# Gate and up products of a feed-forward block as one 2x2 block product: seven block products for eight in two of four k groups, weight sums on VectorE, one PSUM pool

## The chip, the cores and the metric

One core of one Trainium2 chip runs the whole kernel as one program. The metric is the device time of one execution in microseconds; before the change its median is 2232.03 us.

## The reference, cut to what matters

Two transformer-like blocks work on 256 tokens of width 2048, in float32. The first is an attention block with three branches (in the reference `first_block`), the second a recurrent block with a retention branch, and it ends in a feed-forward part. Only that feed-forward part matters here. With `u` the normed activations (256 x 2048, gain `ln2` on each feature) it computes

```python
h = silu(u @ w_gate) * (u @ w_up)      # both weights 2048 x 5632
x = x + h @ w_down                     # 5632 x 2048, then a last norm
```

The factor 1/rms of a token is applied after the products (`hr3`, `hr33`), so that the products themselves take `x * ln2`.

## The kernel before, in words

All large products go through one helper, `gemm` (from L133): the output is token-major, two PSUM tiles of 128 tokens x 512 columns (`ps[0]`, `ps[1]`), and the weights stream past in chunks of 512 columns. For each group of four k tiles of 128 rows one DMA on the SP queue brings `raw` (128 x 4 x 512, 1 MB, three buffers). Each float32 operand is split in two float32r parts: for two k tiles at a time ScalarE (ACT) copies `raw` to `hi` (L162, 128 x 1024), VectorE (DVE) computes `lo = raw - hi` (L163, 128 x 1024). Below, such a pair of tiles is called a part; `hi` and `lo` have four buffers each. The left side is split in the same way into tiles with h and l at the end of their names (class `Lhs`, for this stage `lu2`, tiles u20h, u20l to u23h, u23l). A block product (128 tokens x 128 k x 512 columns) is three matmuls: L141 with hi and high, L142 with lo and high, L143 with hi and low. A part therefore feeds 2 k tiles x 2 token halves x 3 = 12 matmuls, a chunk of 512 columns with 16 k tiles 96.

Between the steps of a product, `issue` takes one piece of side work from a queue (transposes, norms, attention pieces). The frame then schedules all instructions by its own priorities and cost model, so that the order on an engine is not the order of the code: DMA issues run ahead, and an engine goes through its list strictly in order.

The feed-forward part (from L881) runs in three parts of 4, 4 and 3 chunks f of 512 columns. Before the change, for each f: `pg = gemm("fg", w_gate, ...)`; ACT forms tanh (L904, `th`), DVE forms `sg = (th + 1) * pg` (L905); then `pu = gemm("fu", w_up, ...)` and DVE multiplies (L908); `next_lhs` transposes `sg` on TensorE (PE; L216, tiles `trm`, eight transposes a chunk) and splits it to ff0h, ff0l and so on (L203, L204). After each part of chunks four products `fd` with `w_down` follow, and DVE adds them to the residual (L918). What is called a chunk below is one f, gate and up together: 192 matmuls and eight transposes.

PSUM has eight banks: four in the pool `mmp` for `gemm`, two in `trp` for transposes, two in `scp` for attention scores. SBUF slots of 4 KB per partition (`slot`, 28 of them) hold the long-lived tiles.

Of the kernel before, what the change touches and what calls it, by code (L numbers as in the profile page):

```python
# [34 lines left out]
# columns of the shape constants  # L35
# [9 lines left out]
def two_blocks(ctx: ExitStack, tc: tile.TileContext, x, xT, mem, memT, w_in, w_mem_kv, w_proj_a,  # L45
# [69 lines left out]
    class Lhs:  # L115
        """Split transposed activations: chunks of four k-tiles, [P, 4, S] high and low parts."""
# [16 lines left out]
    def gemm(name, w, r0, nk, col0, lhs, fine=False, tail=False, rate=1):  # L133
        ps = [mmp.tile([P, 512], F32, tag="mm", name=name) for _ in range(NT)]
# [49 lines left out]
    def rstd_from(ss, name, r=None):  # L184
        # ss [P, n, NCH] -> (mean + eps) ** -0.5, [P, n]
# [91 lines left out]
    def evac_T(ps, r, dst):  # L277
        # token-major chunk scaled by r, transposed: [P feature, 4, S]
# [16 lines left out]
    def evac_silu(ps, hr, name):  # L295
        # silu(r z) without the factor r / 2
# [37 lines left out]
    def prob_tile(name):  # L334
        return tp.tile([P, 768], F32, tag="prob", name=name)
# [4 lines left out]
    def inverse(l, hr, shape, name):  # L340
        # hr / l, for l [P, 2, NT] or [P, NT]
# [8 lines left out]
    # ================= block 1 =================  # L350
# [6 lines left out]
    # memory attention  # L357
# [21 lines left out]
    def mem_attention(lhs, c):  # L379
# [58 lines left out]
    # causal attention, four heads a group  # L438
# [8 lines left out]
    def causal_attention(hi, lo, c, hp, key):  # L447
# [3 lines left out]
        def scores():  # L451
            sc = scp.tile([P, 2, 512], F32, tag="sc", name="sca")
            for i in range(2):
                h = 2 * hp + i
                nc.tensor.matmul(sc[:, i, 0:P], qa[c][:, h, 0:P], ka[c][:, h, 0:P], start=True, stop=True)
                nc.tensor.matmul(sc[:, i, P:3 * P], qa[c][:, h, P:S], ka[c][:, h, :], start=True, stop=True)
            for i in range(2):
                for b in (0, 2):
# [533 lines left out]
```

## Time and profile before

| what | value |
|---|---|
| median of 2 runs | 2232.03 us (2231.84 to 2232.22) |
| span of the profiled execution, first to last instruction | 2229.9 us |
| what lies around the span, median less span | 2.1 us |
| PE busy in the span | 2212.3 us |
| DVE busy | 1262.8 us |
| ACT busy | 1025.0 us |
| HBM read | 418.00 MB |

The span is that of one profiled execution, and every duration below comes from it. A matmul's recorded duration overlaps with the next one's, so the rate of PE is read from the starts of its rows, not from the mean duration. The same holds, to a smaller degree, for DVE and ACT.

### The profile page before, as it was taken

What the parts mean: (1) busy time and instruction counts of PE and PEld (TensorE: products, weight loads), DVE (VectorE), ACT (ScalarE), POOL (GpSimd) and SP (SyncE); (2) the same over time, 40 slices, a digit from 0 to 9 for tenths busy, and PEclk for the clock granted to TensorE, in tenths of its full rate; (3) what the DMA queues carried; (4) which work ended last, traced back from release to release, by engine and by line L of the source; (5) the groups of instructions that cost most, each with busy time, mean ns of one, the idle gap of its engine ahead of it and who ended that gap; (6) DMA issues with size and microseconds to landing.
All of it is one profiled execution on the core that took longest, in us unless ns stands there. A gap on an engine that the chain in (4) does not pass through costs nothing.

```text
span 2229.9 us, 25130 instructions
## 1 busy us (share of the span) xinstructions
PE 2212.3 (99%) x10108; PEld 1833.4 (82%) x10108; DVE 1262.8 (57%) x1531; ACT 1025.0 (46%) x1253; POOL 9.2 (0%) x15
## 2 busy tenths in 40 slices
PE   8999999999999999999999999999999999999998
PEld 6888888888888888888888888888888888888886
DVE  5545555655555455555677777555555555555555
ACT  6644444444444444444554554544444444434443
POOL 0000000000000000000000000000000000000000
PEclk9999999999999999999999999999999999999999
DMA  8755455455555545556665545555555565565554
GB/s 308 261 185 164 152 189 190 158 181 189 189 189 189 180 143 176 195 191 207 212 226 172 186 152 172 188 188 189 189 189 189 191 194 192 185 198 191 189 198 142
DMA packets 215380, 421.72 MB, mean 189 GB/s; under 512 B 6880, under 2 KB 13152, under 8 KB 215264
## 3 DMA queue, kind: packets, MB, share of 16 engines
q1 hardware_dynamic: 214688, 419.08, 57.2%
q8 instruction: 79, 1.29, 0.2%
q10 hardware_dynamic: 576, 1.05, 0.1%
q14 instruction: 37, 0.30, 0.0%
HBM read 418.00 MB, written 2.10 MB: 188 GB/s over the span
## 4 chain that ended last, share of the span: by engine, by line
PE 98%; DMA 0%; ACT 0%; issue 0%; DVE 0%; SPq 0%; POOLq 0%; POOL 0%; ACTq 0%
PE gate L143 4%; PE gate L142 4%; PE gate L141 4%; PE fg L143 4%; PE fg L141 4%; PE fg L142 4%; PE fu L143 4%; PE fu L141 4%; PE fu L142 4%; PE fd L143 4%; PE fd L141 3%; PE fd L142 3%; PE wo L143 3%; PE wo L141 3%; PE wo L142 3%; PE proj L141 2%
## 5 line engine op out<-in xcount | busy, mean ns | idle before, releaser
L163 DVE TENSOR_TENSOR lo<-raw,hi 128x1024 fp32r<-128x1024 f32 (+1 forms) x769 | 939.5, 1224 | 902.0 <-ACT hi L162 901.0
L162 ACT ACTIVATE hi<-raw 128x1024 fp32r<-128x1024 f32 (+1 forms) x769 | 813.7, 1059 | 1096.9 <-PE fu L143 139.6
L141 PE MATMUL gate<-hi,hn1h 128*128 128x512 f32 x96 | 38.5, 401 | 0.0
L141 PE MATMUL gate<-hi,hn0h 128*128 128x512 f32 x96 | 38.5, 401 | 0.0
L141 PE MATMUL gate<-hi,hn2h 128*128 128x512 f32 x96 | 38.4, 400 | 0.0
L141 PE MATMUL gate<-hi,hn3h 128*128 128x512 f32 x96 | 38.3, 399 | 0.0
L142 PE MATMUL gate<-lo,hn1h 128*128 128x512 f32 x96 | 37.6, 392 | 0.0
L143 PE MATMUL gate<-hi,hn0l 128*128 128x512 f32 x96 | 37.6, 392 | 0.0
L143 PE MATMUL gate<-hi,hn1l 128*128 128x512 f32 x96 | 37.5, 391 | 0.0
L142 PE MATMUL gate<-lo,hn2h 128*128 128x512 f32 x96 | 37.5, 391 | 0.0
L143 PE MATMUL gate<-hi,hn2l 128*128 128x512 f32 x96 | 37.5, 391 | 0.0
L143 PE MATMUL gate<-hi,hn3l 128*128 128x512 f32 x96 | 37.5, 391 | 0.0
L142 PE MATMUL gate<-lo,hn0h 128*128 128x512 f32 x96 | 37.5, 391 | 0.0
L142 PE MATMUL gate<-lo,hn3h 128*128 128x512 f32 x96 | 37.5, 391 | 0.0
L141 PE MATMUL fg<-hi,u20h 128*128 128x512 f32 x88 | 35.2, 400 | 0.0
L141 PE MATMUL fg<-hi,u21h 128*128 128x512 f32 x88 | 35.2, 400 | 0.0
L143 PE MATMUL fg<-hi,u20l 128*128 128x512 f32 x88 | 34.5, 392 | 0.0
L143 PE MATMUL fg<-hi,u21l 128*128 128x512 f32 x88 | 34.4, 391 | 0.0
L142 PE MATMUL fg<-lo,u21h 128*128 128x512 f32 x88 | 34.3, 390 | 0.0
L142 PE MATMUL fg<-lo,u20h 128*128 128x512 f32 x88 | 34.3, 390 | 0.0
L143 PE MATMUL fu<-hi,u20l 128*128 128x512 f32 x88 | 34.3, 390 | 0.0
L143 PE MATMUL fg<-hi,u23l 128*128 128x512 f32 x88 | 34.3, 390 | 0.0
(943 smaller groups left out, 5516.0 us busy)
## 6 DMA issues: line engine op xcount, KB each, us to landing
raw<-in_w_in_dram SPq DMA_DIRECT2D x184, 1024.0 KB, 5.2
raw<-in_w_gate_dram SPq DMA_DIRECT2D x44, 1024.0 KB, 5.2
raw<-in_w_up_dram SPq DMA_DIRECT2D x44, 1024.0 KB, 5.2
raw<-in_w_down_dram SPq DMA_DIRECT2D x44, 1024.0 KB, 5.1
raw<-in_w_out_dram SPq DMA_DIRECT2D x32, 1024.0 KB, 5.1
raw<-in_w_mem_kv_dram SPq DMA_DIRECT2D x15, 1024.0 KB, 7.6
raw<-in_w_proj_m_dram SPq DMA_DIRECT2D x8, 1024.0 KB, 5.1
raw<-in_w_proj_a_dram SPq DMA_DIRECT2D x8, 1024.0 KB, 5.1
```

Source lines behind the costliest of these rows:

```text
L141: nc.tensor.matmul(ps[t], xh[:, c], hi, start=(kt == 0), stop=False)
L142: nc.tensor.matmul(ps[t], xh[:, c], lo, start=False, stop=False)
L143: nc.tensor.matmul(ps[t], xl[:, c], hi, start=False, stop=(kt == nk - 1))
L162: A.activation(hi[:, a:b], raw[:, h + a:h + b], AF.Copy)
L163: V.tensor_tensor(out=lo[:, a:b], in0=raw[:, h + a:h + b], in1=f32(hi[:, a:b]), op=ALU.subtract)
```

## The change

The outputs of a chunk f are seen as a 2 x 2 matrix of blocks: token half 0 or 1 by gate or up. In a k group of kind S two k tiles at a time form a 2 x 2 x 2 block product, and this is computed with seven block products instead of eight (the scheme of Strassen and Winograd), with sums and differences on both sides. On the activation side these are formed once, before the feed-forward part (`next_forms`: seven blocks of 128 x 128 per pair of k tiles). On the weight side they are formed for each chunk on DVE: `t1`, `t2`, `t3`, `t4`, each 128 x 1024. All seven weight forms are split into hi and lo. In a k group of kind D there are eight block products as before, but accumulated so that they fit the same banks: bank 3 takes `x0 - x1` (tile `u21d`, `u23d`) times up. The kinds of the four groups are S, D, S, D (`PATTERN`). The seven products have a PSUM bank each; DVE combines them at the end of a chunk with seven operations of 128 x 512 (L322 to L328), and ACT copies one bank (`p1`, L321). All PSUM tiles come from one pool of eight banks; `raw` has four buffers instead of three, there are 26 slots instead of 28, and score tiles are two single banks, so that some reductions and exponentials of the attention stages are two instructions instead of one.

The core of the diff (comments that it removes, and hunks that only rename a PSUM tile, are left out):

```diff
-NSLOT = 28
+NSLOT = 26
+RBUFS = 4
+TBUFS = 2
+PATTERN = "SDSD"
...
-    mmp = ctx.enter_context(tc.tile_pool(name="mmp", bufs=4, space=bass.MemoryType.PSUM))
-    scp = ctx.enter_context(tc.tile_pool(name="scp", bufs=1, space=bass.MemoryType.PSUM))
-    trp = ctx.enter_context(tc.tile_pool(name="trp", bufs=2, space=bass.MemoryType.PSUM))
+    pp = ctx.enter_context(tc.tile_pool(name="pp", bufs=8, space=bass.MemoryType.PSUM))
...
-            raw = wp.tile([P, 4, 512], F32, tag="raw", name="raw", bufs=3)
+            raw = wp.tile([P, 4, 512], F32, tag="raw", name="raw", bufs=RBUFS)
...
+        def piece(h):
+            k1, k2 = 2 * h, 2 * h + 1
+            a = a_tile("fa", 8)
+            order = (((1, k1), (0, k1), (0, k2), (1, k2)) if kind == "S" else
+                     ((0, k1), (1, k1), (0, k2), (1, k2)))
+            ty = transposed("trm", [block(t, k) for t, k in order])
+            for i, k in ((0, k1), (1, k2)):
+                A.activation(flat(a[:, 2 * i:2 * i + 2]), ty[:, i * S:(i + 1) * S], AF.Copy, scale=gains[:, k:k + 1])
+            if kind == "S":
+                for o, i0, i1 in ((4, 0, 3), (5, 1, 4), (6, 2, 5), (7, 0, 1)):
+                    V.tensor_tensor(out=a[:, o], in0=a[:, i0], in1=a[:, i1], op=ALU.subtract)
+                split(tiles[h][0][:, 0:7], tiles[h][1][:, 0:7], a[:, 1:8])
+            else:
+                V.tensor_tensor(out=a[:, 4:6], in0=a[:, 0:4:2], in1=a[:, 1:4:2], op=ALU.subtract)
+                split(flat(tiles[0][:, k1:k1 + 2]), flat(tiles[1][:, k1:k1 + 2]), flat(a[:, 0:4]))
+                split(tiles[2][:, 0, k1:k1 + 2], tiles[2][:, 1, k1:k1 + 2], a[:, 4:6])
...
+    def gemm2(name, wa, ca, wb, cb, lhs, c11, c21):
...
+            nc.tensor.matmul(ps[b], xh, hi, start=first, stop=False)
+            nc.tensor.matmul(ps[b], xh, lo, start=False, stop=False)
+            nc.tensor.matmul(ps[b], xl, hi, start=False, stop=(left[b] == 0))
...
+        def seven(tiles, ra, rb):
+            def form(b, src):
+                hi, lo = two_parts(src)
+                for h in range(2):
+                    product(b, tiles[h][0][:, FORM[b]], tiles[h][1][:, FORM[b]], hi[:, h], lo[:, h])
+
+            b11, b21, b12, b22 = ra[:, 0::2], ra[:, 1::2], rb[:, 0::2], rb[:, 1::2]
+            t1 = tp.tile([P, 2, 512], F32, tag="prob", name="t1", bufs=TBUFS)
+            form("1", b11)
+            V.tensor_tensor(out=t1, in0=b11, in1=b12, op=ALU.add)
+            form("2", b21)
+            form("5", t1)
+            side()
+            t3 = plus("t3", b12, b22)
+            form("3", b22)
+            t2 = plus("t2", t1, b22)
+            side()
+            form("7", t3)
+            side()
+            form("6", t2)
+            t4 = plus("t4", t2, b21)
+            form("4", t4)
+            side()
+
+        def direct(tiles, ra, rb, last):
+            xh, xl, xd = tiles
+            for raw, banks in ((ra, "24"), (rb, "53")):
+                parts = []
+                for h in range(2):
+                    parts.append(two_parts(raw[:, 2 * h:2 * h + 2]))
+                    side()
...
+                steps = [(b, k) for b in banks for k in range(4)] if last else [(b, k) for k in range(4) for b in banks]
+                for b, k in steps:
+                    hi, lo = parts[k // 2]
+                    product(b, x(b, k, 0), x(b, k, 1), hi[:, k % 2], lo[:, k % 2])
+
+        p1 = v = w = None
+        for q, kind in enumerate(kinds):
+            ra, rb = [wp.tile([P, 4, 512], F32, tag="raw", name="raw", bufs=RBUFS) for _ in range(2)]
+            for raw, wt, c in ((ra, wa, ca), (rb, wb, cb)):
+                nc.sync.dma_start(raw, wt[q * 512:(q + 1) * 512, c:c + 512].rearrange("(k p) n -> p k n", p=P))
...
+            if left["1"] == 0 and p1 is None:
+                p1, v, w = w512("p1"), w512("vv"), w512("ww")
+                A.activation(p1, ps["1"], AF.Copy)
+                V.tensor_tensor(out=v, in0=ps["6"], in1=p1, op=ALU.subtract)
+                V.tensor_tensor(out=w, in0=ps["7"], in1=v, op=ALU.add)
+        V.tensor_tensor(out=c11, in0=ps["2"], in1=p1, op=ALU.add)
+        V.tensor_tensor(out=c21, in0=ps["4"], in1=w, op=ALU.subtract)
+        V.tensor_tensor(out=v, in0=ps["5"], in1=v, op=ALU.add)
+        V.tensor_tensor(out=w, in0=ps["5"], in1=w, op=ALU.add)
+        V.tensor_tensor(out=v, in0=ps["3"], in1=v, op=ALU.add)
+        return v, w
...
-            pg = gemm("fg", w_gate, 0, KD, f * 512, lu2)
+            sg = tp.tile([P, NT, 512], F32, tag="thg", name="sg", bufs=1)
+            ups = gemm2("gu", w_gate, f * 512, w_up, f * 512, lu2, sg[:, 0], sg[:, 1])
             need("r3")
...
-                A.activation(th, pg[t], AF.Tanh, scale=hr3[:, t:t + 1])
-                V.scalar_tensor_tensor(out=sg[:, t], in0=th, scalar=1.0, in1=pg[t], op0=ALU.add, op1=ALU.mult)
-            pu = gemm("fu", w_up, 0, KD, f * 512, lu2)
-            for t in range(NT):
-                V.scalar_tensor_tensor(out=sg[:, t], in0=pu[t], scalar=hr33[:, t:t + 1], in1=sg[:, t],
+                A.activation(th, sg[:, t], AF.Tanh, scale=hr3[:, t:t + 1])
+                V.scalar_tensor_tensor(out=sg[:, t], in0=th, scalar=1.0, in1=sg[:, t], op0=ALU.add, op1=ALU.mult)
+                V.scalar_tensor_tensor(out=sg[:, t], in0=ups[t], scalar=hr33[:, t:t + 1], in1=sg[:, t],
                                        op0=ALU.mult, op1=ALU.mult)
```

In the rows below the numbers after the names are buffer counters; the numbers in brackets are the semaphores that an instruction waits for. The kernel after has its split at L360 (hi) and L361 (lo), and its sums at L275 and L333.

The first place is DVE within a chunk of gate and up. Before, it holds the lo of one part after another:

```order
L163 TENSOR_TENSOR lo_11559<-raw_11556,hi_11558 128x1024 [waits DMAHW4_49,Activation_49]
L163 TENSOR_TENSOR lo_11575<-raw_11556,hi_11574 128x1024 [waits Activation_49]
L163 TENSOR_TENSOR lo_11593<-raw_11590,hi_11592 128x1024 [waits DMAHW5_49,Activation_49]
L163 TENSOR_TENSOR lo_11609<-raw_11590,hi_11608 128x1024 [waits Activation_49]
L163 TENSOR_TENSOR lo_11633<-raw_11630,hi_11632 128x1024 [waits DMAHW6_49,Activation_49]
L163 TENSOR_TENSOR lo_11656<-raw_11630,hi_11655 128x1024 [waits Activation_49]
```

After, the same engine in the second S group (the third k group) of a chunk; raw_11621 is of gate, raw_11622 of up:

```order
L275 TENSOR_TENSOR t1_11625<-raw_11621,raw_11622 128x1024 [waits DMAHW3_49,DMAHW2_49]
L361 TENSOR_TENSOR lo_11627<-raw_11621,hi_11626 128x1024 [waits Activation_49]
L333 TENSOR_TENSOR t3_11657<-raw_11622 128x1024
L361 TENSOR_TENSOR lo_11638<-raw_11621,hi_11637 128x1024 [waits Activation_49]
L361 TENSOR_TENSOR lo_11648<-t1_11625,hi_11647 128x1024 [waits Activation_49]
L361 TENSOR_TENSOR lo_11660<-raw_11622,hi_11659 128x1024 [waits Activation_49]
L361 TENSOR_TENSOR lo_11672<-t3_11657,hi_11671 128x1024 [waits Activation_49]
L333 TENSOR_TENSOR t2_11669<-t1_11625,raw_11622 128x1024 [waits DVE_49]
L333 TENSOR_TENSOR t4_11691<-t2_11669,raw_11621 128x1024 [waits DVE_49]
L361 TENSOR_TENSOR lo_11682<-t2_11669,hi_11681 128x1024 [waits Activation_49]
L361 TENSOR_TENSOR lo_11694<-t4_11691,hi_11693 128x1024 [waits Activation_49]
```

An S group has seven lo and four sums on DVE where two groups of gate and up had four lo before; both raw tiles of the pair must have landed before its first sum.

The second place is DVE at the border from one chunk to the next. Before, around the end of the up product:

```order
L163 TENSOR_TENSOR lo_11681<-raw_11678,hi_11680 128x1024 [waits DMAHW7_49,Activation_49]
L908 SCALAR_TENSOR_TENSOR sg_11479<-fu_11486,hr33_11009,sg_11479 128x512 [waits PE_49]
L908 SCALAR_TENSOR_TENSOR sg_11479<-fu_11487,hr33_11009,sg_11479 128x512 [waits PE_49]
L163 TENSOR_TENSOR lo_11697<-raw_11678,hi_11696 128x1024 [waits Activation_49]
L163 TENSOR_TENSOR lo_11715<-raw_11712,hi_11714 128x1024 [waits DMAHW0_49,Activation_49]
L204 TENSOR_TENSOR ff1l_11627<-trm_11648,ff1h_11626 128x512 [waits Activation_49]
```

After, from the first combination of banks; lo_11799 and lo_11811 already belong to the next chunk's first S group:

```order
L324 TENSOR_TENSOR sg_11449<-gu2_11471,p1_11703 128x512 [waits PE_49]
L275 TENSOR_TENSOR t1_11797<-raw_11793,raw_11794 128x1024 [waits DMAHW7_49,DMAHW6_49]
L325 TENSOR_TENSOR sg_11449<-gu4_11546,ww_11705 128x512 [waits DVE_49,PE_49]
L1069 SCALAR_TENSOR_TENSOR sg_11449<-th_11782,sg_11449 128x512 [waits Activation_49]
L361 TENSOR_TENSOR lo_11799<-raw_11793,hi_11798 128x1024
L326 TENSOR_TENSOR vv_11704<-gu5_11482,vv_11704 128x512 [waits PE_49]
L327 TENSOR_TENSOR ww_11705<-gu5_11482,ww_11705 128x512 [waits DVE_49]
L1069 SCALAR_TENSOR_TENSOR sg_11449<-th_11786,sg_11449 128x512 [waits Activation_49]
L361 TENSOR_TENSOR lo_11811<-raw_11793,hi_11810 128x1024
L328 TENSOR_TENSOR vv_11704<-gu3_11502,vv_11704 128x512 [waits DVE_49,PE_49]
L1070 SCALAR_TENSOR_TENSOR sg_11449<-ww_11705,hr33_11081,sg_11449 128x512 [waits DVE_49]
L1070 SCALAR_TENSOR_TENSOR sg_11449<-vv_11704,hr33_11081,sg_11449 128x512 [waits DVE_49]
```

Between two lo of the next chunk there now stand up to four operations that combine the banks of the chunk before.

## Rows read from the trace of the kernel before

**Rows 1.** Page, span and busy time of each engine with share and instructions.

```profile
span 2229.9 us, 25130 instructions
PE 2212.3 (99%) x10108; PEld 1833.4 (82%) x10108; DVE 1262.8 (57%) x1531; ACT 1025.0 (46%) x1253; POOL 9.2 (0%) x15
```

**Rows 2.** Page, the chain that ended last, by engine.

```profile
PE 98%; DMA 0%; ACT 0%; issue 0%; DVE 0%; SPq 0%; POOLq 0%; POOL 0%; ACTq 0%
```

**Rows 3.** Waits of PE, whole span: us in total, times, longest us.

```profile
PE mk L141 <- ACT mn0h L206: 6.0, 1, 6.0
PE mk L142 <- DVE lo L163: 1.3, 2, 0.8
PE mk L141 <- ACT hi L162: 1.0, 2, 0.7
```

**Rows 4.** Tiles fg, fu, fd: duration ns min/median/max, first and last start us.

```profile
L141 PE MATMUL fg<-hi,u20h x88: 389/390/477, 1490.8 to 2115.2; 128*128 128x512 f32 x88
...
L141 PE MATMUL fu<-hi,u20h x88: 388/389/390, 1513.6 to 2137.4; 128*128 128x512 f32 x88
...
L141 PE MATMUL fd<-hi,ff0h x32: 389/390/476, 1668.8 to 1739.8; 128*128 128x512 f32 x32
```

**Rows 5.** Timeline of PE, second chunk: start us, us, instruction.

```profile
1558.02 0.39 PE L141 MATMUL fu<-hi,u20h 128*128 128x512 f32 x1
...
1579.78 0.39 PE L141 MATMUL fg<-hi,u20h 128*128 128x512 f32 x1
```

**Rows 6.** Windows, one chunk: us, busy of PE, PEld, DVE, ACT, POOL, clock, DMA.

```profile
1535.35:1579.78 44.43, 44.43 (x202) 36.82 (x200) 23.48 (x23) 19.20 (x20) 0.00 (x0) 1.00 0.61 190
```

**Rows 7.** Groups by form on DVE: count, busy us, mean ns, idle before.

```profile
L163 DVE TENSOR_TENSOR lo<-raw,hi 128x1024 fp32r<-128x1024 f32 x767 | 938.1, 1225 | 899.9 <-ACT hi L162 898.9
L908 DVE SCALAR_TENSOR_TENSOR sg<-fu,hr,sg 128x512 f32<-128x512 f32 x22 | 15.4, 744 | 0.0
...
L530 DVE TENSOR_TENSOR mg<-mg,br 128x512 f32<-128x512 f32 x16 | 10.4, 685 | 0.0
```

**Rows 8.** Timeline of DVE, three stretches: start us, us, instruction, idle before it.

```profile
1154.40 0.42 DVE L732 TENSOR_TENSOR lq<-la 128x256 f32<-128x256 f32 x1
1154.92 0.43 DVE L733 SCALAR_TENSOR_TENSOR lq<-lq,lr 128x256 f32<-128x256 f32 x1
...
1180.70 0.68 DVE L321 TENSOR_TENSOR ra<-rq,rrc 128x512 f32<-128x512 f32 x1
1181.30 0.41 DVE L322 TENSOR_TENSOR rb<-rq,rrs 128x256 f32<-128x256 f32 x1
...
1184.56 2.36 DVE L163 TENSOR_TENSOR lo<-raw,hi 128x1024 fp32r<-128x1024 f32 x2
...
1578.35 1.23 DVE L163 TENSOR_TENSOR lo<-raw,hi 128x1024 fp32r<-128x1024 f32 x1 [1.49 <-ACT hi L162]
1579.49 1.40 DVE L908 SCALAR_TENSOR_TENSOR sg<-fu,hr,sg 128x512 f32<-128x512 f32 x2
```

**Rows 9.** ACT: the group of hi by form, and one of them on the timeline.

```profile
L162 ACT ACTIVATE hi<-raw 128x1024 fp32r<-128x1024 f32 x767 | 812.4, 1060 | 1094.8 <-PE fu L143 139.6 <-PE fd L143 134.3 <-PE gate L143 131.9
...
1555.50 1.06 ACT L162 ACTIVATE hi<-raw 128x1024 fp32r<-128x1024 f32 x1 [1.66 <-PE fg L143]
```

**Rows 10.** DMA issues of one weight: count, KB each, us to landing.

```profile
raw<-in_w_gate_dram SPq DMA_DIRECT2D x44, 1024.0 KB, 5.2
```

**Rows 11.** Timeline of PE at the kernel's start, with waits between matmuls.

```profile
8.34 0.63 PE L143 MATMUL mk<-hi,mn0l 128*128 128x512 f32 x1
8.76 0.63 PE L141 MATMUL mk<-hi,mn0h 128*128 128x512 f32 x1
...
12.60 0.50 PE L142 MATMUL mk<-lo,mn0h 128*128 128x512 f32 x1 [0.76 <-DVE lo L163]
12.93 0.39 PE L143 MATMUL mk<-hi,mn0l 128*128 128x512 f32 x1
13.16 0.40 PE L141 MATMUL mk<-hi,mn0h 128*128 128x512 f32 x1
```

More of the change, by code (lines that the diff above doesn't have):

```diff
@@ L71, in f32, with bank @@
         return ap.bitcast(F32)
+    def bank(name, shape=(P, 512)):
+        return pp.tile(list(shape), F32, tag="ps", name=name)
     urgent = deque()
@@ L133, in gemm @@
     def gemm(name, w, r0, nk, col0, lhs, fine=False, tail=False, rate=1):
-        ps = [mmp.tile([P, 512], F32, tag="mm", name=name) for _ in range(NT)]
+        ps = [bank(name) for _ in range(NT)]
         n_tail = 8 if tail else 0
@@ L177, in gemm, with __init__, add, __call__ @@
         return ps
+    FORM = {"1": 0, "2": 1, "4": 2, "5": 3, "6": 4, "3": 5, "7": 6}
+    class Forms:
+        def __init__(self):
+            self.chunks = []
+        def add(self, kind, name):
+            if kind == "S":
+                tiles = [[slot([P, 8, P], f"{name}{x}", F32R) for x in "hl"] for _ in range(2)]
+            else:
+                tiles = [slot([P, 4, S], f"{name}{x}", F32R) for x in "hl"]
+                tiles.append(slot([P, 2, 4, P], f"{name}d", F32R))
+            key = f"{name}#{len(done)}#{len(queue)}#{len(urgent)}#{len(self.chunks)}"
+            self.chunks.append((kind, tiles, key))
+            return self.chunks[-1]
+        def __call__(self, q):
+            need(self.chunks[q][2])
+            return self.chunks[q]
@@ new lines, in gemm2, with product, two_parts, side @@
+    def gemm2(name, wa, ca, wb, cb, lhs, c11, c21):
+        kinds = [c[0] for c in lhs.chunks]
+        assert kinds[0] == "S" and kinds[-1] == "D"
+        left = {b: 2 * kinds.count("S") + (4 * kinds.count("D") if b in "2345" else 0) for b in "1234567"}
+        ps = {}
+        def product(b, xh, xl, hi, lo):
+            first = b not in ps
+            if first:
+                ps[b] = bank(name + b)
+            left[b] -= 1
+            nc.tensor.matmul(ps[b], xh, hi, start=first, stop=False)
+            nc.tensor.matmul(ps[b], xh, lo, start=False, stop=False)
+            nc.tensor.matmul(ps[b], xl, hi, start=False, stop=(left[b] == 0))
+        def two_parts(src):
+            hi = wp.tile([P, 2, 512], F32R, tag="hi", name="hi")
+            lo = wp.tile([P, 2, 512], F32R, tag="lo", name="lo")
+            split(hi, lo, src)
+            return hi, lo
+        def side():
+            if urgent or queue:
+                issue()
+        def seven(tiles, ra, rb):
[27 more added lines that the diff above has]
+                    side()
+                def x(b, k, part):
+                    if b == "3":
+                        return xd[:, part, k]
+                    t = 0 if b == "2" else 1
+                    return (xh, xl)[part][:, k, t * P:(t + 1) * P]
+                steps = [(b, k) for b in banks for k in range(4)] if last else [(b, k) for k in range(4) for b in banks]
[7 more added lines that the diff above has]
+                nc.sync.dma_start(raw, wt[q * 512:(q + 1) * 512, c:c + 512].rearrange("(k p) n -> p k n", p=P))
+            tiles = lhs(q)[1]
+            if kind == "S":
+                seven(tiles, ra, rb)
+            else:
+                direct(tiles, ra, rb, q == len(kinds) - 1)
+            if left["1"] == 0 and p1 is None:
[9 more added lines that the diff above has]
+        return v, w
@@ L180, in square_sum, with plus @@
+    def plus(name, a, b):
+        t = tp.tile([P, 2, 512], F32, tag="prob", name=name, bufs=TBUFS)
+        V.tensor_tensor(out=t, in0=a, in1=b, op=ALU.add)
+        return t
     def square_sum(src, acc):
@@ L384, in scores @@
         def scores():
-            sc = scp.tile([P, 2, NT, S], F32, tag="sc", name="scm")
+            sc = [bank("scm", (P, NT, S)) for _ in range(2)]
             for i in range(2):
@@ L551, in scores @@
                 st["l"] = small([P, NT], "lb")
-            sc = scp.tile([P, 2, 512], F32, tag="sc", name="scb")
+            sc = {k + 1 - t: bank("scb") for k in range(t + 1)}
             for k in range(t + 1):
@@ L857, in two_blocks @@
     h1 = x1
-    lu2 = Lhs()
+    lu2 = Forms()
     ss3 = small([P, NT, NCH], "ss3", 1)
```

77 lines of the change are left out of this document (46 added, 31 removed).

## Prediction

> **What bounds the kernel now.** I read the page's head first: PE is busy for 99% of the span [rows 1]; then the chain that ended last, 98% of it PE [rows 2]; then who PE waits for: in the whole span only 8.3 us, all in `mk`, at the start [rows 3]. So the kernel before is a row of matmuls without gaps, and a change pays only by taking matmuls away, as long as no other engine becomes late. How dense the row is, the timeline shows: the 96 matmuls of one up product take 1579.78 - 1558.02 = 21.76 us, 0.2267 us from start to start [rows 5]; the mean of 0.39 us in a group overstates that. A chunk, gate and up, takes 1558.02 - 1513.6 = 44.4 us [rows 4, 5]: 192 x 0.2267 = 43.5 and 0.9 for its eight transposes. The first part of four chunks lasts from 1490.8 to 1668.8, 178.0 us [rows 4]. The second has 3 x 44.4 + 43.5 = 176.7 (the last chunk's transposes fall into the down product), the third 132.3. Gate and up together: 487.0 us of the 2229.9.
>
> The engine to watch is DVE: 23.48 us busy in a chunk of 44.43, ACT 19.20 [rows 6]. DVE's lo instructions are 1225 ns each and mostly wait, 899 us in all, for ACT's hi [rows 7], which in turn waits for PE to free a buffer, 1.66 us in the row shown [rows 9]: both run ahead of PE until the four buffers are full, then keep its step.
>
> **What goes.** An S group has 14 block products instead of 16; two S groups take 4 of 64 from a chunk, 12 of 192 matmuls, 132 in the 11 chunks: 132 x 0.2267 = 29.9 us. That is all that can be won: 1.3%. PE then needs 180 x 0.2267 + 0.9 = 41.7 us a chunk.
>
> **What comes, on DVE.** Back to back, a 128x1024 instruction costs 1.14 us from start to start, not 1.225: L908 starts 1.14 after the lo before it, and two lo in a row take 2.36 [rows 8]. A 128x512 one costs 0.60 (1180.70 to 1181.30 [rows 8]), an L908-like one with a scalar 0.66. The sums t1 to t4 are not in the trace; the nearest row is lo itself, two float32 operands of the same shape from SBUF, and an addition like L530 has 685 ns for half of it [rows 7], 0.60 from start to start by the same 0.085 of overlap. I take 1.14; the lower end is the same, the upper 1.33 (recorded length plus 0.1 where the next depends on it, as 1154.40 + 0.42 to 1154.92 shows [rows 8]). A chunk now has:
> - 22 lo for 16 (7 + 4 + 7 + 4): 25.1 us
> - 8 sums: 9.1 us
> - L322 to L328, seven of 128x512: 4.2 us
> - L1069 and L1070, two each: 2.5 us; two lo of `ff`: 1.2 us
>
> That makes 42.1 us, against PE's 41.7 and 23.48 before. DVE is now as full as PE. It is also uneven: an S group needs 12.5 us of DVE for 42 x 0.2267 = 9.5 of PE, a D group 4.6 for 10.9. ACT's hi grows to 22 x 1.06 = 23.3 us a chunk [rows 9]: no bound.
>
> **The lag within a chunk.** I laid DVE's order after the change beside PE's, with time 0 where PE starts the first D group and DVE has just delivered its first part.
> - DVE: three lo to 3.4, t1 to 4.6, lo, t3, lo to 8.0. Now the four buffers stop it: the third D part is read until 8.2, then 0.2 for the tail of its last matmul, then ACT's 1.06, so the next lo starts at 9.5, the one after, by the fourth part (10.9), at 12.2. DVE stands still for about 3 us here, though it has too much to do. The rest of this S group ends at 19.5.
> - PE: D group to 10.9, S group to 20.9 (9.5 and about 0.5 of waiting for the hi of t4), second D group to 31.7.
> - DVE from 19.5 on never waits: four lo, L322 and L323 to 25.2; five combinations, four `sg` operations, two lo of `ff`, the next S group's eleven and the next D group's first lo are 4.2 + 1.3 + 1.2 + 12.5 + 1.1 = 20.4 more, with 0.1 for each of four that depend on the one before: 46.0. A matmul after a wait costs 0.1 more (12.60 to 12.93 where the spacing is 0.23 [rows 11]); two of these delay a buffer: 46.2.
>
> So a chunk that follows another takes 46.2 us instead of 44.4. PE passes its first S group in 46.2 - 31.7 = 14.5 us instead of 9.5 + 0.9; the combination of the chunk before stands between the lo it waits for (L326 to L1070).
>
> **Sum.** Where a chunk opens a part, no combination is ahead of it and the buffers are full: its first S group takes 9.8 after `fd`, and 12.4 for the very first chunk, where the residual updates and the last forms of u23 (about 4 us on DVE) come between. After: first S groups 12.4 + 9.8 + 9.8, eight borders at 46.2 = 369.6, three last stretches of 31.7: 496.7 us for 487.0, so 9.7 us more. On the profiled execution that is 2229.9 + 9.7 = 2239.6 of span; with the 2.1 around it, and as median, **2242 us**, 0.4% slower: no change that can be told, since about 2% (45 us) is what can be.
>
> **Costed at nothing.** At the end of a part the combination lies beside `fd`, where a part feeds 12 matmuls, 2.72 us, for 1.14 of DVE. Forms of u20 to u22 lie beside `wo2`. Before the feed-forward part PE's order is nearly unchanged; the split reductions and exponentials are small additions on engines that nobody waits for there [rows 3]. Without that cover some forty at 0.3 us would be 12 us. Fewer slots and the pool move nothing on PE. Transfers: gate's raw is issued when t2 of the S group before is done, up's when t4 is, 3.5 us before time 0; 5.2 us to landing [rows 10] gives 1.7. If both share the queues (190 GB/s at a share of 0.61 [rows 6], so 311 at most, 3.4 us for each) it is 5.1, and t1 is 1.7 late, which the 3 us of standstill absorb.
>
> **Rivals.**
> - *PE sets the pace.* If DVE's standstill doesn't occur (looser buffers than I count), a chunk takes DVE's 42.1 and a little: 11 x 42.2, and 2 for the first, are 466: 21 less, 2211; at the very best 2202. For it: DVE has only 0.4 more work than PE. Against: the buffers, which ACT waits for already [rows 9]. Chance 0.18.
> - *DVE holds each instruction* (slower). If in a saturated stretch each of 43 instructions starts only after the recorded end of the last, 43 x 0.085 = 3.7 us are added: 49.9 a chunk, 8 x 3.7 = 30 more, 2272. With 0.1 for noticing ACT's semaphore before each of 30, 52.9, 2296. Break-even with before is a chunk of 45.0; 2% slower begins at 50.6. For it: 0.1 to 0.2 of idle stands before many lo; against: the 2.36 for two. Chance 0.15, half of it beyond 2%. [...] The trace's lo, which have waits, start 0.09 before the recorded end where the wait is over.
> - *Raw lands late.* If the pair takes 8 us or more, a chunk gains about 3: 2266. Chance 0.07.
> - *The clock falls.* [...] PE now waits at every border. [...] Against: with waits of 0.7 us at 12 us the spacing is back to 0.23 [rows 11]. Chance 0.05. [...]
>
> **How the numbers follow.** Forecast 0.55 (2230 to 2256, chunks of 45 to 48); the rest as above. Faster by over 2% would need 45 us, more than the matmuls' 29.9: 0.01. Slower by over 2%: half of the second rival, most of the clock's, a little of the third: 0.12. Within: 0.87. The range of 2212 to 2272 cuts off the best end of the first rival and the far ends of the others.
>
> **What would show it.** PE's matmuls fewer by 132; in gate and up DVE at 90% or more, with waits of PE on lo in the first S group of a chunk (about 4 us a border) and DVE waiting for hi in the first D group; a period of 46.2 from one chunk's first `gu1` to the next's. It is wrong if the period is under 44 or over 48, if PE waits for raw, or if the clock shows under 1.00.

## The result, and the profile after

The changed kernel takes 2255.35 us, median of 2 runs (2254.68 to 2256.01), for 2232.03: a ratio of 1.0104 with an interval of 1.0087 to 1.0121. It is 1.0% slower. The forecast was 2242: the sign and the stated range hold, but the loss is 23.3 us where 9.7 were forecast.

The page's head and its chain by engine answer to [rows 1, 2]:

```profile
span 2254.2 us, 25296 instructions
PE 2207.5 (98%) x9976; PEld 1810.8 (80%) x9976; DVE 1483.0 (66%) x1796; ACT 1101.3 (49%) x1350; POOL 10.2 (0%) x15
PE 86%; DVE 10%; ACT 2%; issue 2%; DMA 0%; SPq 0%; ACTq 0%; POOLq 0%; POOL 0%; DVEq 0%
```

PE has 10108 - 9976 = 132 matmuls fewer, as the change says, and the span is 24.3 us longer. DVE now holds 10% of the chain, where it had nothing. The waits of PE over the whole span (us in total, times, longest) answer to [rows 3]:

```profile
PE gu L252 <- ACT hi L360: 24.6, 37, 1.0
PE mk L145 <- ACT mn0h L363: 6.2, 1, 6.2
PE gu L253 <- DVE lo L361: 3.4, 10, 0.6
PE trp L373 <- ACT proba L629: 1.5, 1, 1.5
PE mk L146 <- DVE lo L167: 1.0, 2, 0.5
```

Two rows are new in gate and up. The larger names ACT's hi, but ACT is half idle: the hi that PE waits for is mostly one of t2 or t4, and ACT itself waits for DVE to form the sum (42 times, 62.6 us in all). This is ACT at the second border, between chunk 1 and chunk 2 (start, us, in brackets the idle time before):

```profile
1593.01 1.06 ACT L360 ACTIVATE hi<-t 128x1024 fp32r<-128x1024 f32 x1 [3.67 <-DVE t L333]
1594.29 1.06 ACT L360 ACTIVATE hi<-t 128x1024 fp32r<-128x1024 f32 x1 [0.22 <-DVE t L333]
```

The starts of the four k groups of chunk 1, and of the first two of chunk 2, are on PE's timeline:

```profile
1536.86 0.39 PE L252 MATMUL gu<-hi,u20h 128*128 128x512 f32 x1
...
1551.39 0.39 PE L252 MATMUL gu<-hi,u21h 128*128 128x512 f32 x1
...
1562.27 0.39 PE L252 MATMUL gu<-hi,u22h 128*128 128x512 f32 x1
...
1572.62 0.39 PE L252 MATMUL gu<-hi,u23h 128*128 128x512 f32 x1
...
1583.49 0.39 PE L252 MATMUL gu<-hi,u20h 128*128 128x512 f32 x1
...
1599.58 0.43 PE L252 MATMUL gu<-hi,u21h 128*128 128x512 f32 x1
```

The differences are 14.53, 10.88, 10.35 and 10.87: a chunk of 46.63 us, for 46.2 forecast and 44.43 before [rows 6]. But the next first S group takes 16.09. What differs is PE's pace. The second border's four waits, and the rows behind them:

```profile
1589.39 0.50 PE L252 MATMUL gu<-hi,u20h 128*128 128x512 f32 x1 [0.52 <-ACT hi L360]
...
1591.71 0.50 PE L253 MATMUL gu<-lo,u20h 128*128 128x512 f32 x1 [0.30 <-DVE lo L361]
...
1594.12 0.50 PE L252 MATMUL gu<-hi,u20h 128*128 128x512 f32 x1 [0.99 <-ACT hi L360]
1595.40 0.50 PE L252 MATMUL gu<-hi,u20h 128*128 128x512 f32 x1 [0.78 <-ACT hi L360]
1595.74 0.39 PE L253 MATMUL gu<-lo,u20h 128*128 128x512 f32 x1
...
1596.59 0.63 PE L253 MATMUL gu<-lo,u20h 128*128 128x512 f32 x1
1597.02 0.63 PE L254 MATMUL gu<-hi,u20l 128*128 128x512 f32 x1
```

From 1596.59 to 1597.02 a matmul takes 0.43 us instead of 0.2267. The windows (us; busy of PE, PEld, DVE, ACT, POOL; granted clock; DMA) of the first border, of the second and of the stretch behind its waits, and of chunk 1 as a whole:

```profile
1536.00:1552.00 16.00, 13.33 (x58) 9.70 (x57) 15.88 (x17) 9.44 (x11) 0.00 (x0) 1.00 0.28 96
1583.49:1596.20 12.71, 10.03 (x43) 6.95 (x42) 12.59 (x14) 6.22 (x7) 0.00 (x0) 1.00 0.16 44
1596.20:1599.60 3.40, 3.40 (x10) 2.63 (x9) 3.40 (x4) 2.10 (x3) 0.00 (x0) 0.50 1.05 401
1536.86:1583.49 46.63, 43.47 (x189) 34.28 (x188) 43.02 (x44) 25.39 (x27) 0.00 (x0) 1.00 0.52 180
```

The granted clock is 0.50 behind the second border's waits, where matmuls start 0.43 us apart, and it is 1.00 at the first border. By the same differences of starts, the first border of each of the three parts of chunks takes 14.53 to 14.58 and the five later ones 16.09 to 16.12: 1.57 us more at each of five, 7.9 us. The four waits are the same at all eight, to 0.02 us. DVE is 43.02 us busy in the chunk, 92%, for 23.48 before.

Where DVE still stands idle is the first D group, as forecast:

```profile
1558.44 1.22 DVE L361 TENSOR_TENSOR lo<-raw,hi 128x1024 fp32r<-128x1024 f32 x1
1560.89 1.23 DVE L361 TENSOR_TENSOR lo<-t,hi 128x1024 fp32r<-128x1024 f32 x1 [1.23 <-ACT hi L360]
1563.61 1.23 DVE L361 TENSOR_TENSOR lo<-raw,hi 128x1024 fp32r<-128x1024 f32 x1 [1.50 <-ACT hi L360]
1564.97 1.23 DVE L361 TENSOR_TENSOR lo<-t,hi 128x1024 fp32r<-128x1024 f32 x1
1566.23 2.49 DVE L333 TENSOR_TENSOR t<-t,raw 128x1024 f32<-128x1024 f32 x2
```

1.23 + 1.50 = 2.7 us of standing still, and only then, at 1566.23, t2 and t4. Why they come so late is what the experiments settle.

Adding up, from the starts of gu's first group and of fd in each part of chunks: gate and up take 187.6 + 185.4 + 137.2 = 510.2 us, 22.6 more than before by the same starts (487.5) [rows 4]; fd is unchanged, and gate and up begin 1.6 later (1492.4 for 1490.8).

### The profile page after: what moved, and what is told of

It is laid out like the page before. It is cut to its first block, busy times and chain, and to the rows that moved or that the text cites. A ratio compares the mean times of both kernels' runs of the same rounds, so it can differ in the third digit from the quotient of the medians.

```text
span 2254.2 us, 25296 instructions
## 1 busy us (share of the span) xinstructions
PE 2207.5 (98%) x9976; PEld 1810.8 (80%) x9976; DVE 1483.0 (66%) x1796; ACT 1101.3 (49%) x1350; POOL 10.2 (0%) x15
## 4 chain that ended last, share of the span: by engine, by line
PE 86%; DVE 10%; ACT 2%; issue 2%; DMA 0%; SPq 0%; ACTq 0%; POOLq 0%; POOL 0%; DVEq 0%
PE gate L147 4%; PE gate L145 4%; PE gate L146 4%; DVE lo L361 4%; PE fd L146 3%; PE fd L145 3%; PE fd L147 3%; PE gu L253 3%; PE gu L254 3%; PE gu L252 3%; DVE t L333 3%; PE wo L147 3%; PE wo L145 3%; PE wo L146 3%; PE proj L147 2%
## 5 line engine op out<-in xcount | busy, mean ns | idle before, releaser
L167 DVE TENSOR_TENSOR lo<-raw,hi 128x1024 fp32r<-128x1024 f32 (+1 forms) x593 | 722.8, 1222 | 648.4 <-ACT hi L166 647.0
L166 ACT ACTIVATE hi<-raw 128x1024 fp32r<-128x1024 f32 (+1 forms) x593 | 626.9, 1058 | 830.5 <-PE gate L147 122.5
L360 ACT ACTIVATE hi<-raw 128x1024 fp32r<-128x1024 f32 x154 | 158.5, 1054 | 104.5 <-PE gu L254 76.7
L361 DVE TENSOR_TENSOR lo<-raw,hi 128x1024 fp32r<-128x1024 f32 x154 | 185.0, 1219 | 33.0 <-ACT hi L360 33.0
L360 ACT ACTIVATE hi<-t 128x1024 fp32r<-128x1024 f32 x88 | 93.3, 1060 | 108.4 <-DVE t L333 62.6
L361 DVE TENSOR_TENSOR lo<-t,hi 128x1024 fp32r<-128x1024 f32 x88 | 107.7, 1224 | 22.9 <-ACT hi L360 20.3
L252 PE MATMUL gu<-hi,u20h 128*128 128x512 f32 x154 | 66.4, 431 | 19.2 <-ACT hi L360 19.2
L253 PE MATMUL gu<-lo,u20h 128*128 128x512 f32 x154 | 66.4, 431 | 3.5 <-DVE lo L361 2.8
L252 PE MATMUL gu<-hi,u22h 128*128 128x512 f32 x154 | 61.2, 397 | 5.4 <-ACT hi L360 5.4
L254 PE MATMUL gu<-hi,u20l 128*128 128x512 f32 x154 | 63.6, 413 | 0.0
L333 DVE TENSOR_TENSOR t<-t,raw 128x1024 f32<-128x1024 f32 x44 | 53.9, 1225 | 1.4
```

Source lines behind the costliest of these rows:

```text
L166: A.activation(hi[:, a:b], raw[:, h + a:h + b], AF.Copy)
L167: V.tensor_tensor(out=lo[:, a:b], in0=raw[:, h + a:h + b], in1=f32(hi[:, a:b]), op=ALU.subtract)
L252: nc.tensor.matmul(ps[b], xh, hi, start=first, stop=False)
L253: nc.tensor.matmul(ps[b], xh, lo, start=False, stop=False)
L254: nc.tensor.matmul(ps[b], xl, hi, start=False, stop=(left[b] == 0))
L333: V.tensor_tensor(out=t, in0=a, in1=b, op=ALU.add)
```

## The experiments

In all of them the split stays at L360 and L361 unless a row says otherwise. Three theories were open. *Work*: DVE has 42.1 us of work a chunk against PE's 41.7, and no slack for what the border adds. *Chain*: the sums wait for their own two buffers. *Clock*: part of the loss is PE's pace after the waits.

**1. The sums left out.** The forms that took t1 to t4 are split from raw blocks; the output is not the reference's.

```diff
-            V.tensor_tensor(out=t1, in0=b11, in1=b12, op=ALU.add)
-            form("5", t1)
+            form("5", b12)
...
-            t3 = plus("t3", b12, b22)
-            form("7", t3)
+            form("7", b12)
```

(and the same for t2 and t4). 

> Leaves out the eight weight sums of a chunk on DVE (forms 5, 7, 6, 4 split a raw block in place of a sum), so the gate and up products are not those of the reference; every matmul, split and combination stays. DVE then needs 42.1 - 9.1 = 33.0 us a chunk. Theory 1 (DVE's backlog at a border makes PE wait, and a longer wait brings the clock down): the first S group of a following chunk falls from 14.5 to 16.1 us to about 10.4, the second from 10.3 to 9.5, no stretch shows a clock of 0.5, a chunk takes 41.7 to 42.5; gate and up together 459 to 467 us instead of 510, the whole 2204 to 2212 us. Rival (PE waits at a border for PSUM banks that the combination has not yet freed, or for raw): the first S group stays at 13 or more, the whole at 2240 or more.

2202.76 us (2202.57 to 2202.9), ratio 0.9869 [0.9855, 0.9884], just under the expected 2204 to 2212. No row of gu is left among PE's waits. The window of one chunk:

```profile
1533.81:1575.54 41.73, 41.73 (x189) 34.58 (x188) 34.01 (x36) 25.92 (x27) 0.00 (x0) 1.00 0.58 202
```

PE's 41.7 us of the forecast is the floor, and it is reached once DVE has 9 us less. So the matmuls saved are real (29.3 us of the 29.9), and what is lost on top of that is lost through the eight sums, about 1 us of run 3 aside. This run takes away the work of the sums and their buffers together; runs 7 to 12 tell the two apart.

**2. The waits filled.** Matmuls without use stand in the first S group of a chunk that follows another, eight ahead of form 6 and three ahead of form 4, where PE waits; the form then starts its bank anew.

```diff
+                if again:
+                    for _ in range({"6": 8, "4": 3}.get(b, 0)):
+                        nc.tensor.matmul(ps[b], prev[-1][0], prev[-1][1], start=True, stop=True)
```

> Adds eleven matmuls to the first S group of each chunk that follows another (eight ahead of form 6, three ahead of form 4, into the bank that the form then starts anew), 88 in all, 2.5 us of PE work a border at 0.2267 each; they use a part that is already there, and nothing is computed from them. If the clock's fall costs 1.6 us at five of eight borders because PE stands idle there, and DVE sets the pace: the added matmuls lie in the 4 us of waits and cost nothing, the borders with 16.1 fall to 14.5, no stretch shows 0.5, the whole is 2247. If the fall has another cause: 2255 or a little more, with eight matmuls at 0.43 us as before. If PE sets the pace at a border after all: 88 x 0.2267 = 20 us more, 2275.

2247.88 us (2247.63 to 2248.14), ratio 1.0072 [1.0055, 1.0089]: with 88 matmuls more it is 7.5 us faster. In this trace all eight borders take 14.53 to 14.56; the second, which took 16.09:

```profile
1583.38:1597.94 14.56, 13.84 (x62) 10.51 (x61) 14.44 (x16) 8.08 (x9) 0.00 (x0) 1.00 0.26 86
```

No window of a border shows a clock under 1.00 any more. So here the clock falls because PE idles in the border, and that is worth 7.5 us, close to 5 x 1.57 = 7.9. DVE's pace is untouched, 43.01 us busy in the chunk that begins at 1583.38 for 43.02 in chunk 1 of the changed kernel: the rest of the loss is not the clock's.

**3. The pools alone.** One PSUM pool, four raw buffers, 26 slots and single-bank score tiles as in the changed kernel; gate and up by `gemm` as before. 

> Takes over from the change only the one PSUM pool, four raw buffers, 26 slots and the single-bank score tiles; gate and up are eight block products for eight, as before. Theory: the 1.6 us by which gate and up start later after the change (1492.4 for 1490.8) come from the attention stage, where PE waits 1.5 us for proba, and these edits alone give 2233.6. Rival 1: the 1.6 comes with the forms of the activations beside wo2: 2232.0. Rival 2: the fourth raw buffer or the pool changes gate and up as well: outside 2231 to 2235.

2233.09 us (2232.87 to 2233.3), ratio 1.0005 [0.9996, 1.0014]. It has one wait that the kernel before lacks, and that the changed kernel shares:

```profile
PE trp L373 <- ACT proba L629: 1.5, 1, 1.5
```

In this trace gate and up begin at 1492.3, 1.5 later than before. So about 1 us of the loss comes from ahead of the feed-forward part; the interval of the ratio, which includes 1, would allow for none at all.

**4. D groups outside.** The border then meets D groups, which ask DVE for less than half as much (4.6 us for 12.5 by the forecast's count).

```diff
-PATTERN = "SDSD"
+PATTERN = "DSSD"
```

> The same work with the kinds of the k groups in the order D, S, S, D instead of S, D, S, D. DVE's 42.1 us a chunk stay. Theory 1: the combination of the chunk before (8.2 us of DVE) now lies beside a D group, 8.2 + 4.6 of DVE for 10.9 of PE, a lag of about 2 us; the two S groups in a row need 25.0 of DVE for 19.0 of PE, less a lead of up to four parts, so PE waits some 2 to 4 us there, in smaller pieces. A chunk 43 to 45 us, no clock of 0.5, the whole 2233 to 2248. Rival (the waits only move, since DVE needs as much as PE in any order, and the buffers stop it in the second D group as long): a chunk of 46 or more, 2250 to 2258.

2293.11 us (2292.26 to 2293.47), ratio 1.0274 [1.0258, 1.0289]: a loss outside what was expected. PE's waits show a new one:

```profile
PE gu L252 <- ACT hi L360: 25.0, 44, 0.8
PE trm L373 <- DVE sg L1070: 24.8, 8, 3.1
```

Two S groups in a row leave DVE so far behind that PE reaches the transposes before the combination (L1070) is done, 3.1 us at each of eight borders. Some 16 us of the 38 more than the changed kernel are the clock's again, by the differences of starts: the first D group of chunk 2, for one, takes 13.06 us at a granted clock of 0.83 where the same group takes 11.00 at 1.00. SDSD is the better order, and the border is not bound to the S group that stands first: what is late moves on to whatever comes next.

**5. t3 on GpSimd.** 22 sums leave DVE.

```diff
-            t3 = plus("t3", b12, b22)
+            t3 = plus("t3", b12, b22, nc.gpsimd)
```

> Only t3, one of the four sums of an S group, goes to GpSimd; 2.3 us of DVE's 42.1 a chunk leave it. Theory 1 (DVE's backlog at a border sets the time): the first S group of a following chunk falls by t3's 1.14 us, from 14.5 to 13.4, the second from 10.3 to 10.0 or less; a chunk 45.0 to 45.3 and the clock's falls (1.6 us at five of eight borders) fewer: the whole 2238 to 2250, whatever one sum costs on GpSimd up to about 5 us. Rival (GpSimd at work slows DVE's two-operand instructions): lo while t3 runs takes clearly over 1.22 us, the border stays at 14.5 or longer, the whole 2253 or more.

2260.36 us (2258.26 to 2263.74), ratio 1.0128 [1.0113, 1.0143]. The 22 sums on the page, and GpSimd and DVE at one time:

```profile
L333 POOL TENSOR_TENSOR t<-raw 128x1024 f32<-128x1024 f32 x22 | 72.0, 3275 | 713.3 <-DMA raw<-in_w_up_dram 626.5
```
```profile
1529.83 2.41 POOL L333 TENSOR_TENSOR t<-raw 128x1024 f32<-128x1024 f32 x1 [17.56 <-DMA raw<-in_w_up_dram]
...
1530.05 3.27 DVE L275 TENSOR_TENSOR t<-raw 128x1024 f32<-128x1024 f32 x1
```

The t1 beside it takes 3.27 us on DVE where the changed kernel shows 1.22: 2.05 lost for an instruction of 1.14 saved. The trace has 21 such DVE instructions beside the 22 sums, each a t1 or a lo of raw with 2.6 to 3.4 us; they are 42 us longer in all, for 25 saved. The outcome is the rival's: first S groups take 14.9 us or more, and at three of them the clock falls.

**6. All four sums on GpSimd** (`nc.gpsimd` in all four places). 

> All eight sums of a chunk on GpSimd, none on DVE. If a sum takes up to about 3 us there and doesn't slow DVE, GpSimd needs 24 of 42 us a chunk and DVE 33.0: the time nears that of the kernel without sums, 2203 to 2225. Rival: the chain t1, t2, t4 with two buffers takes longer than an S group of PE (9.5 us), so PE waits for hi of t2 and t4 at every S group, 22 times 3 us or more: 2250 to 2330, with DVE idle before lo of t2 and t4.

2330.11 us (2326.47 to 2332.66), ratio 1.0438 [1.0421, 1.0456]. The lo of DVE by form, and PE's first wait:

```profile
L361 DVE TENSOR_TENSOR lo<-raw,hi 128x1024 fp32r<-128x1024 f32 x154 | 253.9, 1673 | 32.0 <-ACT hi L360 31.6
L361 DVE TENSOR_TENSOR lo<-t,hi 128x1024 fp32r<-128x1024 f32 x88 | 131.9, 1499 | 87.8 <-ACT hi L360 87.3
```
```profile
PE gu L253 <- DVE lo L361: 49.3, 33, 3.2
```

A lo of raw takes 1673 ns instead of 1219 in the mean, a lo of a sum 1499 instead of 1224: 94 us in all, nearly the 100 (88 x 1.14) that DVE no longer spends on sums. The rival's sign is there as well, 87.3 us of DVE idle before the lo of sums, and the granted clock is 0.95 from the first gate product to the last down products (1490 to 2252 us), where the changed kernel has 0.99 (1490 to 2178 us). The time lies at the upper end of what the rival gave; this run doesn't tell how much each of the three costs.

**7. A third buffer for the sums.** To make room, the tiles tagged `pt` have one buffer.

```diff
-TBUFS = 2
+TBUFS = 3
...
-        return tp.tile([P, 768], F32, tag="pt", name=name)
+        return tp.tile([P, 768], F32, tag="pt", name=name, bufs=1)
```

> A third buffer for the sums (and one instead of two for the transposed probabilities, to make room), so that t2 and t4 need not wait until t1 and t3 are read. Theory 1 (DVE's amount of work between the standstill and the end of the border sets a chunk): the waits of PE for the hi of t2 and t4 (1.0 and 0.8 us) go, but as many come before lo, and a chunk stays at 46 to 46.6 without the clock; the second S group falls from 10.3 to about 9.5 and the first grows by as much; the whole 2244 to 2256, by how often the clock falls. Rival (the chain t1, t2, t4 through two buffers sets the border): the first S group falls to 12.7, a chunk to 44.0, the whole 2230 to 2236.

2233.13 us (2232.8 to 2233.44), ratio 1.0006 [0.9996, 1.0015]: 22 us of the 23 are gone with one buffer. By the starts of the two traces about 8 of them are the clock's, 9.8 come from the eight chunks that follow another (1.2 each) and 5.8 from the three that open a part; gate and up begin 1.0 later. The total is the rival's. A chunk, and DVE in its first D group:

```profile
1535.19:1580.60 45.41, 42.99 (x189) 34.38 (x188) 42.90 (x44) 25.89 (x28) 0.00 (x0) 1.00 0.56 185
```
```profile
1557.21 1.22 DVE L333 TENSOR_TENSOR t<-t,raw 128x1024 f32<-128x1024 f32 x1
1558.83 1.23 DVE L361 TENSOR_TENSOR lo<-t,hi 128x1024 fp32r<-128x1024 f32 x1 [0.39 <-ACT hi L360]
1560.08 1.23 DVE L333 TENSOR_TENSOR t<-t,raw 128x1024 f32<-128x1024 f32 x1
1561.54 1.23 DVE L361 TENSOR_TENSOR lo<-raw,hi 128x1024 fp32r<-128x1024 f32 x1 [0.23 <-ACT hi L360]
```

t2 and t4 now run at 1557.21 and 1560.08, in the time in which DVE stood still before; of 2.7 us of standing 0.39 + 0.23 are left in these rows. The second S group drops from 10.35 to 9.52, its matmuls alone, and the clock is 1.00 in the chunk. Yet a chunk still takes 45.4, neither the rival's 44.0 nor theory 1's 46 or more: DVE is busy for 42.90 of it.

**8. Five hi and lo instead of four**, and three raw instead of four to make room (`wp` with `bufs=5`, `RBUFS = 3`), with two sum buffers. 

> Five buffers for hi and lo instead of four, and three for raw instead of four, to make room. Theory 1: DVE's standstill of about 3 us in the first D group, which four buffers make, gets 1.1 to 2 us shorter, and a chunk that follows another 44.5 to 45.5: the whole 2232 to 2245. Rival (three raw buffers are too few, since an S group holds two until its last sum): DVE waits for raw before t1 or before the D group's lo, in rows, and a chunk takes 47 or more: 2258 and up.

2239.75 us (2238.58 to 2245.47), ratio 1.004 [1.0025, 1.0055]. The first border, the third, at which the clock holds, and the chunk that begins with the third:

```profile
1535.01:1550.99 15.98, 12.87 (x51) 9.78 (x50) 15.75 (x17) 7.76 (x9) 0.00 (x0) 0.89 0.37 119
1629.92:1643.72 13.80, 11.19 (x52) 8.64 (x50) 13.67 (x15) 6.20 (x8) 0.00 (x0) 1.00 0.30 99
1629.92:1675.00 45.08, 42.47 (x190) 34.54 (x188) 42.67 (x44) 25.13 (x27) 0.00 (x0) 1.00 0.58 197
```

The total is theory 1's. Second S groups take 9.52 here too (one 9.63), and the chunk at the full clock is 45.08 for 45.41 in run 7. So a buffer more for the parts or one more for the sums, either ends PE's waits in the second S group. DVE's standstill itself is not gone here: in the chunk that begins at 1629.92 it idles for 1.29 and 0.56 us where it was 1.23 and 1.50. What makes this version slower than run 7 is the clock, which falls at four of its eight borders (15.4 to 16.4 us, the others 13.8).

**9 to 12. Versions.** Four more tell whether DVE's amount of work is the last cause, and whether a version beats both kernels. With one S group (`PATTERN = "SDDD"`) DVE has about 34 us of work and PE 43.1. Number 9 is that alone, number 10 has three sum buffers as well (as in 7), number 11 is SDSD with three sum buffers and five parts (7 and 8 together), number 12 is all three edits.

> PATTERN is SDDD: one S group in a chunk instead of two, two buffers for the sums as in the changed kernel. PE then has 186 matmuls and eight transposes a chunk, 43.1 us; DVE 19 lo, 4 sums and the combination, about 34 us. Theory 1 (over a whole chunk DVE has as much to do as PE, so what the border costs is never made good): with 9 us of slack DVE is far ahead when the border comes, first S groups after a chunk take 10.4 to 12, no fall of the clock, 2217 to 2230 us. Rival (the border by itself, the combination and the chain t1, t2, t4 through two buffers, costs the same whatever DVE had to do before): first S groups of 14.3 to 14.6, 8 x 4 = 32 us above the floor of 2217, 2245 to 2252 us.

> SDDD with three buffers for the sums (and one for the tiles tagged pt, to make room). Theory 1: as with one S group alone, or up to 5 us less, 2217 to 2225 us. Rival: the chain through two buffers is gone, the combination is left: first S groups of 12.8 as in the run with three buffers and two S groups, 8 x 2.4 = 19 us above the floor of 2217, 2234 to 2238 us.

> SDSD with three buffers for the sums and five for hi and lo (three for raw, one for pt). Theory 1 (with both chains loose only DVE's 42.1 us of work stand against PE's 41.7): a chunk of 42.2 to 43.5, 2205 to 2220 us. Rival (the fifth part only moves the standstill, since raw now has three buffers and a pair needs two; the chunk stays at 45.4 as with three sum buffers alone): 2230 to 2238 us.

> SDDD with three buffers for the sums and five for hi and lo (three for raw, one for pt): the one-S version that ran at 2226.9 us with one more part of lead. Theory 1 (its borders of 11.4 us stand over the 10.5 of matmuls and transposes only because DVE's lead is four parts): borders of 10.5 to 10.8, 2218 to 2222 us. Rival (raw, three buffers where a pair takes two, lands too late in D groups, as DVE waited 10 us for it in the run with two S groups): no gain or a loss, 2225 to 2232 us.

| run | us (lowest to highest) | ratio to before, interval | chunk 1, us |
|---|---|---|---|
| 9, SDDD | 2233.93 (2233.52 to 2234.84) | 1.0009 [1.0, 1.0019] | 44.62 |
| 10, SDDD, three sums | 2226.89 (2225.89 to 2228.51) | 0.9979 [0.9969, 0.9988] | 44.00 |
| 11, SDSD, three sums, five parts | 2227.68 (2225.38 to 2229.55) | 0.9981 [0.9972, 0.999] | 44.26 |
| 12, SDDD, three sums, five parts | 2218.6 (2218.2 to 2218.84) | 0.994 [0.9926, 0.9953] | 43.10 |

The windows of chunk 1 in number 9, 11 and 12, each from its own trace:

```profile
1537.67:1582.29 44.62, 43.68 (x195) 35.62 (x194) 35.05 (x37) 22.92 (x24) 0.00 (x0) 1.00 0.58 189
```
```profile
1534.79:1579.05 44.26, 42.41 (x190) 34.49 (x189) 41.58 (x43) 25.32 (x27) 0.00 (x0) 1.00 0.58 190
```
```profile
1536.02:1579.12 43.10, 43.10 (x196) 35.71 (x195) 34.72 (x37) 22.86 (x24) 0.00 (x0) 1.00 0.59 196
```

Number 9 lies between the two expectations: with 9.6 us of idle time on DVE a chunk still takes 1.5 more than PE's 43.1, so the two buffers cost something by themselves. Number 10 is 2 us above the upper end of theory 1 and below the rival. Number 11 lies between its two expectations as well: with both buffers loose DVE is busy for 41.58 of 44.26, and it also waits for raw, which has three buffers now:

```profile
DVE t L275 <- DMA raw<-in_w_up_dram: 10.0, 13, 1.5
```

At one of its eight borders the clock falls too: 0.50 from 2071.34 to 2074.07.

Number 12 is as expected. PE is busy for all 43.10 us of the chunk, no row of gu is among its waits, and 13.4 us are gained on the kernel before. That is nearly all that one S group can give: 6 matmuls in each of 11 chunks, 66 x 0.2267 = 15.0, less the 1 us of run 3. It beats both kernels. With the same buffers one S group is faster than two each time: 2233.9 for 2255.4 (numbers 9 and the changed kernel), 2226.9 for 2233.1 (10 and 7), 2218.6 for 2227.7 (12 and 11). Half the matmuls saved bring more than all of them: DVE then keeps 8 us of slack in 43.

## Why the prediction was wrong in its size, step by step

- *What goes*: right. 132 matmuls; PE's floor of 41.7 us a chunk is 41.73 in run 1.
- *DVE's ledger and the durations*: right. The sums, which the trace of before did not show, have 1218 to 1225 ns; instructions start 1.13 to 1.14 us apart where they are not held, and 0.60 to 0.66 for the halves:

```profile
1584.52 0.74 DVE L1070 SCALAR_TENSOR_TENSOR sg<-ww,hr,sg 128x512 f32<-128x512 f32 x1
1585.18 0.74 DVE L1070 SCALAR_TENSOR_TENSOR sg<-vv,hr,sg 128x512 f32<-128x512 f32 x1
1585.84 1.22 DVE L361 TENSOR_TENSOR lo<-t,hi 128x1024 fp32r<-128x1024 f32 x1
1586.97 1.22 DVE L333 TENSOR_TENSOR t<-raw 128x1024 f32<-128x1024 f32 x1
```

  With that the rival by which DVE holds each instruction falls: 46.6 us a chunk at the full clock, not 49.9. What the prediction said for it, 0.1 to 0.2 of idle before many lo, was a misreading: in the trace of before only 44 of the 769 lo have so short an idle time before them (0.06 to 0.26 us). And for the 0.1 of noticing ACT's semaphore the trace has 0.03: the hi that starts at 1555.50 and has 1.06 us [rows 9] ends at 1556.56, and the lo that waits for it starts at 1556.59.
- *The lag within a chunk*: right in kind and near in size. First S groups of 14.53 to 14.58 at the full clock for 14.5 forecast, a standstill of 2.7 for about 3. Mis-sized: the second S group, 10.0 with "about 0.5 of waiting", took 10.3 to 10.35, eleven times 0.33, 3.6 us.
- *The clock*: the step that failed. The sum took the granted clock of 1.00 throughout and left a fall to a rival with a chance of 0.05, because at the kernel's start a wait of 0.7 us at 12 us did not bring one [rows 11]. But a border is not one wait. In four of them, 0.52, 0.30, 0.99 and 0.78 of idle time in the trace's rows, PE falls 14.53 - 10.46 = 4.1 us behind by the starts (10.46 is the same group in run 1). At five of eight borders the clock then fell to 0.50. The rival was right that PE's waits bring the clock down: some eight matmuls ran at the lower level, 0.43 us apart, 1.57 us a border. 5 x 1.57 = 7.9; run 2 says 7.5. But the 0.12 for slower by over 2%, 45 us, counts most of this rival's chance, and no run of the changed kernel shows such a price. The prediction had named this as a sign of being wrong, a clock under 1.00, and the five chunks with a fall take 48.2 to 48.3 us, over its limit of 48.
- *First S groups that open a part*: 11.5, 10.3 and 10.3 for 12.4, 9.8 and 9.8, and a first D group of 11.75 for 10.9: together 0.9 more. The eight borders themselves and the D groups, 10.88 each, give about 1.
- *Costed at nothing*: ahead of the feed-forward part the loss is 1.6 us by the starts, 1.1 by run 3 on the medians. There PE does wait once, 1.5 us for ACT's proba, where the prediction had nobody wait.
- *PE sets the pace* was the rival on the fast side, 2211, "if DVE's standstill doesn't occur (looser buffers than I count)". Runs 7 and 8 made the buffers looser: 2233 and 2240, 2228 with both. There DVE is busy for 94% of a chunk, and PE does not set the pace. In run 12, with DVE at 81%, it does.
- *Raw lands late* did not come: DVE waits for raw before a t1 twice in the whole span, 1.6 us in all.

Gate and up: 496.7 forecast, and 7.9 + 3.6 + 0.9 + 1 more are 510.1, for 510.2 measured. So the mechanism was right but for the clock, and most of the missed 13 us is this one neglected effect of a wait that the prediction had right.

One explanation was too narrow. The prediction laid the standstill to the four buffers of hi and lo alone. Run 7 shows that DVE stood there because t2 also had no buffer: t1 and t3 hold both until the lo of t3 is done, which itself waits for a free hi. The order of the instructions showed it, with t2 and t4 behind the lo of t3.

Left open: when a border's waits bring the clock down. In the changed kernel it holds at the first border of each part and falls at the later ones with the same waits; in run 8 it fell at the first border of all and held at the third. Neither what PE misses in sum nor how the waits are cut up decides it: in run 8 the fourth border has waits of 1.35 and 1.23 us and takes 13.80 at a clock of 1.00, the fifth has 1.38 and 1.23 and takes 15.38 at 0.89. In run 7 it held at all eight, with waits of 1.03, 0.86 and 0.45. No run settles the cause.

## What to carry to other kernels

Before work is moved from a full engine to a helper engine, add up the helper's work in the same stretch: where both come out near the length of the stretch, a short standstill of the helper can reach the full engine (here 42.1 us of DVE against PE's 41.7, 2.7 us of standing still, and a chunk of 46.63), and a version that moves half as much can win more (here, with the same buffers, 2218.6 us against 2227.7). Look for what the helper could do while it stands still and which buffer forbids it; one buffer was worth 22 us here, some 8 of them through the clock. And once TensorE is forecast to wait at every step, give the fall of its clock a term of the sum (here 7.9 us of 23), not a small chance beside it.

## What was not expected of the hardware

- Matmuls without use made the kernel faster: 88 of them in PE's waits took 7.5 us off, and the clock then stayed at 1.00.
- An addition of 128x1024 on GpSimd that runs beside one of DVE stretched DVE's from 1.22 to 3.27 us. With the same shape GpSimd's 22 additions take 3.28 us in the mean.
